# Expert layer of a decoder block: half of the experts read as fetched rows, the other half as dense, unsplit tiles

## The chip, the cores and the metric

The kernel runs on one core of one Trainium2 chip. The metric is the device time of one execution in microseconds (us). The kernel before takes 1032.59 us, the median of three runs (1030.81, 1032.59 and 1033.53).

## What is computed

The program is one decoder layer over 256 tokens of 1024 numbers in float32: a conditioning product, a projection, sparse attention beside a short convolution, an output projection, and then the part that the change touches, a retrieval layer over 16,384 single-neuron experts. Its reference, cut to what matters (8 heads, 128 keys in each half, 16 chosen pairs in each head):

```python
q = (hb @ peer_wq).reshape(B, Q_BLOCK, PEER_HEADS, 2, PEER_HALF)
s = einsum('bqhpd,hpnd->bqhpn', q, peer_subkeys)
vals, idx = top_k(s, 16)
combo = vals[..., 0, :, None] + vals[..., 1, None, :]
ids = idx[..., 0, :, None] * 128 + idx[..., 1, None, :]
top_s, pos = top_k(combo, 16)
expert = take_along_axis(ids, pos)
g = softmax(top_s)
a = gelu(einsum('bqhkd,bqd->bqhk', peer_u[expert], hb))
out = einsum('bqhk,bqhkd->bqd', g * a, peer_v[expert])
```

So each token has 128 chosen experts (8 heads by 16), each with a row of 1024 numbers in `peer_u` and one in `peer_v`. An expert's number is i * 128 + j, with i and j the two key positions. Among the 32,768 pairs that the reference's inputs give, 16,030 (49%) have j of 64 or more.

## The kernel before

Everything up to the second norm (attention, convolution, output projection) comes first and is not touched. The expert part follows in four stages.

**Queries.** Sixteen weight tiles of 512 KB go through PE against the normed tokens, held as `h2h` and `h2l`. Float32 accuracy is had by splitting: `split` (L116 to L118) rounds a tile on ScalarE to `hi`, and VectorE subtracts to get `lo`; `mm3` (L120 to L123) then adds up three products. `scores` (L839 to L845) multiplies with the sub-keys, and `top16` (L811 to L830) finds the best 16 on VectorE.

**U.** The kernel is dense: it does not fetch the rows of the chosen experts, but multiplies all tokens with all 128 tiles of `peer_u` (tile j holds the 128 experts with that j), by `u_tile` (L960 to L973): 24 products of 256 columns per tile. ScalarE takes the gelu of each result into a buffer `B0` or `B1`, which holds expert by token. During the first 64 tiles VectorE works through the generator `retrieve` (L805 to L953), which turns scores into the chosen pairs `Ti`, `Tj` and their weights `Tg`.

**G.** During the second 64 tiles `g_tile` (L975 to L995) makes, for four tokens at a time, a one-hot matrix of i on ScalarE (L981, L984) and a weighted one-hot matrix of j on VectorE (L982), multiplies them on PE (L986), and multiplies the result into the buffers (L993). Pairs that were not chosen get the weight zero.

**V.** `v_tile` (L1020 to L1023) multiplies the 128 buffered weight slices, split again, with the 128 split tiles of `peer_v`: 12 products of 512 columns per tile. `finish` (L1025 to L1030) applies the gate, adds the residual and stores.

All tiles come through one queue on SP: `load` (L110), `pump`, `advance`, `fill`, `take`. The engines' own orders come from the order in which the code emits instructions; VectorE's order in the U stage is by budget: after each tile the generator is run until the sum of its yielded estimates passes 1.38 us (L1002 to L1006). Tiles in `FULL` (L38) are taken unsplit: PE multiplies them as plain float32, in two instructions per product (L632, L643).

Of the kernel before, what the change touches and what calls it, by code (L numbers as in the profile page):

```python
# [8 lines left out]
F32 = mybir.dt.float32  # L9
# [26 lines left out]
# Order of the work. Streamed tiles are counted in the order in which they are used.  # L36
# [10 lines left out]
J0 = 64  # L47


def layout(a):  # L50
    """Only moves data: transposes, slices and repeats of the inputs."""
# [31 lines left out]
    o["pu"] = a["peer_u"].reshape(128, 128, KD, 128).transpose(1, 3, 2, 0)  # L83
# [8 lines left out]
def body(tc, i, out):  # L92
# [48 lines left out]
    def advance():  # L141
# [6 lines left out]
        if count[0] in FULL:  # L148
            ahead.append((raw,))
            return  # L150
# [93 lines left out]
    def fold(col, acc, g):  # L244
        """Adds the sums of half of acc over its partitions to a column vector."""
# [23 lines left out]
    def normed(tb):  # L269
        """x times its reciprocal root mean square, tokens on partitions."""  # L270
# [52 lines left out]
    W += [(i["pu"][j].rearrange("p k c -> p (k c)"), None) for j in range(NJ)]  # L323
# [12 lines left out]
    for j in range(NJ):  # L336
        if j >= 16 and j % 8 == 0 and j < 80:
            k = (j - 16) // 8
            queue.append((i["w_ada"][5, k], add_row(gate2, k)))
        queue.append((i["pv"][j], None))  # L340
# [454 lines left out]
    B0 = pool("B0").tile([128, NJ // 2, L], F32, name="B0")  # L795
    tr = pool("tr")
    gw = pool("gw", 2)
    Ti = tr.tile([128, L], F32, name="Ti")
    Tj = tr.tile([128, L], F32, name="Tj")
    Tg = tr.tile([128, L], F32, name="Tg")  # L800
    p2 = ExitStack()
    r1 = p2.enter_context(tc.tile_pool(name="r1", bufs=1))
    r2 = p2.enter_context(tc.tile_pool(name="r2", bufs=2))

    def retrieve():  # L805
        skT = r1.tile([128, 16, 128], F32, name="skT")
        nc.scalar.dma_start(out=skT, in_=i["sk"])
        v16 = [r1.tile([128, 16, 16], F32, name=f"v16{tb}") for tb in range(NT)]
        x16 = [r1.tile([128, 16, 16], U32, name=f"x16{tb}") for tb in range(NT)]

        def top16(items, tag):  # L811
            """items: (values, sorted values out, positions out); chains run side by side."""
            ws = []
            for c, v, x in items:
                nc.vector.max(out=v[:, 0:8], in_=c)
            yield 0.4
            for c, v, x in items:
                nc.vector.max_index(out=x[:, 0:8], in_max=v[:, 0:8], in_values=c)
            yield 0.4
            for n, (c, v, x) in enumerate(items):  # L820
                w = r2.tile([128, c.shape[-1]], F32, name=f"{tag}{n}")
                nc.vector.match_replace(out=w, in_to_replace=v[:, 0:8], in_values=c, imm_value=NEG)
                ws.append(w)
            yield 0.4
            for w, (c, v, x) in zip(ws, items):
                nc.vector.max(out=v[:, 8:16], in_=w)
            yield 0.4
            for w, (c, v, x) in zip(ws, items):
                nc.vector.max_index(out=x[:, 8:16], in_max=v[:, 8:16], in_values=w)
            yield 0.4  # L830

        def stage1(hp, sg):
            return top16([(sg[:, tb], v16[tb][:, hp], x16[tb][:, hp]) for tb in range(NT)], "wv")

        def ready():
            while todo:
                yield from stage1(*todo.pop(0))

        def scores(hp, pqT):  # L839
            ps = p_acc.tile([128, NT, 128], F32, name="acc")  # L840
            for tb in range(NT):
                nc.tensor.matmul(ps[:, tb], pqT[:, tb * 128:tb * 128 + 128], skT[:, hp], start=True, stop=True)  # L842
            sg = r2.tile([128, NT, 128], F32, name="sg", bufs=10)
            nc.scalar.copy(sg, ps)
            todo.append((hp, sg))  # L845

        todo = []
        prev = None
        cur = iter(())
        left = 0.0  # L850
        for hp in range(16):
# [9 lines left out]
            nc.scalar.copy(prev, ps)  # L861
            if hp > 2:
                left += BUDGET1
# [9 lines left out]
        yield 0  # L873
        yield from cur
        yield from ready()
        TB = range(NT)
        vv = [v16[tb].rearrange("p (h z) k -> p h z k", z=2) for tb in TB]
        xf = [r1.tile([128, 16, 16], F32, name=f"xf{tb}") for tb in TB]
        xv = [z.rearrange("p (h z) k -> p h z k", z=2) for z in xf]
        for tb in TB:  # L880
            nc.vector.tensor_copy(xf[tb], x16[tb])
# [42 lines left out]
        for tb in TB:  # L924
            for h in range(H):
                for k in range(16):
# [4 lines left out]
                    if k % 2:  # L931
                        yield 0.37
# [140 lines left out]
```

## Time and profile before

| | |
|---|---|
| runs (us) | 1030.81, 1032.59, 1033.53; median 1032.59 |
| span of the profiled execution | 1031.9 us (its own time is not listed beside the three) |
| PE busy | 991.0 us (96%) |
| VectorE (DVE) busy | 774.2 us (75%) |
| ScalarE (ACT) busy | 595.9 us (58%) |
| GpSimd (POOL) busy | 7.5 us (1%) |
| read from memory | 189.58 MB, 185 GB/s over the span |

The profile's page gives busy time per engine, the span in 40 slices, the chain of work that ended last, and the costliest groups. A busy PE is no proof of PE at its peak, since its instructions overlap: the pace is read from the starts of consecutive instructions. Other views (windows, timeline, groups by shape, DMA issues) cut the same execution into parts.

### The profile page before, as it was taken

The numbers are of one execution on the slowest core, as the hardware profiler recorded it, in microseconds if no ns is written. First come the engines' busy times: TensorE is split into PE (matmuls) and PEld (weight loads), VectorE is DVE, ScalarE is ACT, GpSimd is POOL, SyncE is SP. The second block draws the span as 40 slices with busy tenths as digits, with TensorE's granted clock in tenths as the row PEclk, the third lists the DMA queues.
The fourth block names the chain that finished last, engine by engine and source line by source line (L and its number), as shares of the span: only waits on it lengthen the run. The fifth ranks groups of instructions, "written<-read, shape, count | busy, mean of one in ns | idle before, by whom it ended". The sixth has DMA issues, their size and how long they took to land.

```text
span 1031.9 us, 18401 instructions
## 1 busy us (share of the span) xinstructions
PE 991.0 (96%) x6642; PEld 912.4 (88%) x6642; DVE 774.2 (75%) x2103; ACT 595.9 (58%) x1210; POOL 7.5 (1%) x20
## 2 busy tenths in 40 slices
PE   2599989999999999999999999999999999999998
PEld 2599987899999999999999999988888888888886
DVE  5789687788988999777788888866666666665655
ACT  3354643545445454599888888845454455455452
POOL 1000000000000000000000000000000000000000
PEclk9799998999999999999999999999999999999999
DMA  9686486345655655544444444456677777665663
GB/s 317 223 311 222 171 277 211 98 144 155 181 183 176 190 180 185 184 144 134 141 138 143 144 143 136 136 180 207 214 216 218 210 223 222 202 189 180 198 191 121
DMA packets 52891, 191.82 MB, mean 186 GB/s; under 512 B 6112, under 2 KB 6144, under 8 KB 52672
## 3 DMA queue, kind: packets, MB, share of 16 engines
q1 hardware_dynamic: 52416, 189.30, 58.4%
q8 instruction: 52, 0.85, 0.3%
q10 hardware_dynamic: 144, 1.05, 0.3%
q0 software_dynamic: 240, 0.31, 0.1%
q14 instruction: 39, 0.32, 0.1%
HBM read 189.58 MB, written 1.05 MB: 185 GB/s over the span
## 4 chain that ended last, share of the span: by engine, by line
PE 93%; DVE 4%; DMA 1%; ACT 1%; issue 0%; SPq 0%; ACTq 0%; DVEq 0%
PE acc L121 14%; PE acc L123 14%; PE acc L122 14%; PE mm L121 13%; PE mm L122 13%; PE mm L123 13%; PE pg L986 6%; PE acc L632 2%; DMA raw<-in_w_ada_dram 1%; DVE gate L219 1%; PE acc L842 1%; PE pg L517 1%; DVE acc L219 0%; PE mm L708 0%; ACT hi L117 0%
## 5 line engine op out<-in xcount | busy, mean ns | idle before, releaser
L118 DVE TENSOR_TENSOR lo<-raw,hi 128x1024 fp32r<-128x1024 f32 x302 | 369.1, 1223 | 122.7 <-ACT hi L117 120.3
L117 ACT CAST hi<-raw 128x1024 fp32r<-128x1024 f32 x302 | 316.0, 1047 | 158.1 <-PE mm L122 105.3
L121 PE MATMUL mm<-h2h,hi 128*128 128x256 f32 x1152 | 333.0, 289 | 0.5 <-ACT hi L117 0.4
L122 PE MATMUL mm<-h2l,hi 128*128 128x256 f32 x1152 | 325.9, 283 | 0.0
L123 PE MATMUL mm<-h2h,lo 128*128 128x256 f32 x1152 | 325.8, 283 | 0.0
L121 PEld LDWEIGHTS mm<-h2h,hi 128*128 128x128 f32 x1152 | 220.7, 192 | 0.9 <-ACT hi L117 0.9
L122 PEld LDWEIGHTS mm<-h2l,hi 128*128 128x128 f32 x1152 | 221.0, 192 | 0.0
L123 PEld LDWEIGHTS mm<-h2h,lo 128*128 128x128 f32 x1152 | 220.5, 191 | 0.0
L121 PE MATMUL acc<-hi,wh 128*128 128x512 f32 x512 | 199.7, 390 | 0.0
L123 PE MATMUL acc<-hi,wl 128*128 128x512 f32 x512 | 199.3, 389 | 0.0
L122 PE MATMUL acc<-lo,wh 128*128 128x512 f32 x512 | 199.3, 389 | 0.0
L117 ACT CAST wh<-B 128x256 fp32r<-128x256 f32 x128 | 52.0, 407 | 148.4 <-PE acc L122 145.6
L122 PEld LDWEIGHTS acc<-lo,wh 128*128 128x128 f32 x512 | 96.1, 188 | 20.1 <-issue 0.2
L123 PEld LDWEIGHTS acc<-hi,wl 128*128 128x128 f32 x512 | 96.1, 188 | 20.0
L121 PEld LDWEIGHTS acc<-hi,wh 128*128 128x128 f32 x512 | 96.1, 188 | 20.0 <-issue 0.2
L118 DVE TENSOR_TENSOR wl<-B,wh 128x256 fp32r<-128x256 f32 x128 | 54.2, 424 | 52.4 <-ACT wh L117 51.8
L981 ACT ACTIVATE oi<-iota,Ti 128x128 f32<-128x128 f32 x256 | 88.0, 403 | 0.0
L993 DVE TENSOR_TENSOR B<-pg,B 128x256 f32<-128x256 f32 (+63 forms) x127 | 45.0, 355 | 46.3 <-PE pg L986 46.3
L982 DVE TENSOR_SCALAR oj<-iota,Tj,Tg 128x128 f32<-128x128 f32 x256 | 71.3, 342 | 1.6 <-PE pg L986 1.6
L986 PE MATMUL pg<-oj,oi 128*128 128x128 f32 x512 | 67.6, 275 | 0.0
L986 PEld LDWEIGHTS pg<-oj,oi 128*128 128x128 f32 x512 | 62.8, 192 | 0.0
L928 DVE SCALAR_TENSOR_TENSOR ju<-iota,tf,ce 128x50 f32<-128x50 f32 x256 | 51.7, 266 | 0.0
(220 smaller groups left out, 945.9 us busy)
## 6 DMA issues: line engine op xcount, KB each, us to landing
raw<-in_pu_dram SPq DMA_DIRECT2D x128, 512.0 KB, 3.7
raw<-in_pv_dram SPq DMA_DIRECT2D x128, 512.0 KB, 4.3
raw<-in_w_ada_dram SPq DMA_DIRECT2D x48, 512.0 KB, 5.0
raw<-in_wq_dram SPq DMA_DIRECT2D x16, 512.0 KB, 3.7
raw<-in_w_c_dram SPq DMA_DIRECT2D x12, 512.0 KB, 4.7
raw<-in_w_kv_dram SPq DMA_DIRECT2D x8, 512.0 KB, 5.9
raw<-in_w_out_dram SPq DMA_DIRECT2D x8, 512.0 KB, 5.0
raw<-in_w_iq_dram SPq DMA_DIRECT2D x4, 512.0 KB, 4.8
```

Source lines behind the costliest of these rows:

```text
L117: nc.scalar.copy(hi, src)
L118: nc.vector.tensor_tensor(lo, src, hi.bitcast(F32), op=OP.subtract)
L121: nc.tensor.matmul(ps, a[0], b[0], start=first, stop=False)
L122: nc.tensor.matmul(ps, a[0], b[1], start=False, stop=False)
L123: nc.tensor.matmul(ps, a[1], b[0], start=False, stop=last)
L219: nc.vector.scalar_tensor_tensor(acc[:, s], raw[:, s], sc[:, k:k + 1], acc[:, s], op0=OP.mult, op1=OP.add)
L632: nc.tensor.matmul(ps[0], w[0][:, s], hT[:, k], start=k == 0, stop=k == KD - 1)
L928: nc.vector.scalar_tensor_tensor(ju, iota[:, :NC2], tf[tb][:, h, k:k + 1], ce[tb][:, h], op0=OP.is_equal, op1=OP.mult, accum_out=ef[tb][:, ...
L981: nc.scalar.activation(out=oi[:, n], in_=iota, func=AF.Square, bias=Ti[:, t:t + 1])
L982: nc.vector.tensor_scalar(oj[:, n], iota, Tj[:, t:t + 1], Tg[:, t:t + 1], op0=OP.is_equal, op1=OP.mult)
L986: nc.tensor.matmul(ps[:, n], oi[:, n], oj[:, n], start=True, stop=True)
L993: nc.vector.tensor_tensor(B[:, :m, t], pv[:, j0:j0 + m], B[:, :m, t], op=OP.mult)
```

## The change

Experts with j below 64 stay dense (64 tiles of U, 64 of V), but their tiles are no longer split: PE multiplies the raw float32 tile with one product where there were three. Experts with j of 64 or more are handled by fetched rows.

- `retrieve` now runs for one half of the tokens at a time (tb 0, then tb 1). The look-up of the expert number, 256 small instructions (L928), becomes, for each head, a comparison of 128x800, a product (on GpSimd for tb 0, on VectorE for tb 1) and a sum. It also writes two lists of row numbers, `iu` and `iv`; 65536 is added for pairs with j below 64, which puts them out of bounds, so that their row is not fetched.
- `fetch_u` has GpSimd fetch, for one pair slot of 128 tokens, the 128 rows of `peer_u` (4 KB each); six fetches are kept ahead. `dots` multiplies them with the tokens' own rows and sums, one VectorE instruction over 1024 columns per slot: 256 in all. `weigh` takes the gelu and the weight, `place` puts the result, transposed, on the diagonals of `S`.
- `fetch_v` has GpSimd fetch the 128 chosen rows of `peer_v` for each of four tokens (a quad); two quads are held. `strips` multiplies a quad with its 32-column parts of `S`, four products side by side in four column strips of PE, for each half of the output: 64 quads, 512 products. They add to the same sums as the dense `v_tile`.
- The order is by budget again: 3.5 us of VectorE work are emitted after each dense tile, 1.75 after each quad. By these estimates the lists for tb 0 stand after dense U tile 12, those for tb 1 after tile 48; 46 of the 64 G groups fall among the U tiles and 18 behind them; 48 of the 256 dots are emitted before V; the first quad follows dense V tile 32, one quad then follows each V tile, and 32 quads are left when the dense tiles are through.

The diff, cut to its core:

```diff
+WHOLE = set(FULL) | set(range(53, 53 + 2 * J0))
+SKIP = 65536.0
+U_US, V_US, S_US, G_US = 3.5, 3.5, 1.75, 1.0
-        if count[0] in FULL:
+        if count[0] in WHOLE:
             ahead.append((raw,))
             return
+            for z in (h, h + 1):
+                eng = nc.gpsimd if tb == 0 else nc.vector
+                eq = r2.tile([128, 16, NC2], F32, name="eq", bufs=3)
+                nc.vector.tensor_tensor(eq, iota[...], tf[...], op=OP.is_equal)
+                eng.tensor_tensor(eq, eq, ce[:, z, None].to_broadcast([128, 16, NC2]), op=OP.mult)
+                pend.append((ef[:, z], eq))
+                yield from summed(2)
+        nc.vector.tensor_scalar(off, fi[:, 1], float(J0), SKIP, op0=OP.is_lt, op1=OP.mult)
+        nc.vector.tensor_tensor(off, off, flat(ef), op=OP.add)
+        nc.vector.tensor_copy(iu[tb], off)
+    def fetch_u():
...
+                raw = pp.tile([128, D], F32, name="ug", tag=tag)
+                nc.gpsimd.indirect_dma_start(
+                    out=raw, out_offset=None, in_=i["ur"],
+                    in_offset=bass.IndirectOffsetOnAxis(ap=iu[tb][:, n:n + 1], axis=0),
+                    bounds_check=128 * 128 - 1, oob_is_err=False)
+    def dots():
...
+        nc.vector.tensor_tensor_reduce(out=junk, in0=raw, in1=h2r[:, tb], scale=1.0, scalar=0.0,
+                                       op0=OP.mult, op1=OP.add, accum_out=ad[tb][:, n:n + 1])
+        fetch_u()
+    def stream():
...
+        yield from retrieve(0)
+        other = retrieve(1)
+        for n in range(128):
+            yield dots()
+            for _ in range(2):
+                z = next(other, None)
...
+        weigh(0)
+        for n in range(128):
+            yield dots()
+        weigh(1)
+    def u_tile(j):
...
-            mm3(ps, (w[0][:, s], w[1][:, s]), (h2h[:, k], h2l[:, k]), k == 0, k == KD - 1)
+            nc.tensor.matmul(ps, w[0][:, k * 128:k * 128 + 128], h2f[:, k], start=k == 0, stop=k == KD - 1)
+    for j in range(J0):
+        ps = u_tile(j)
...
+        g_step()
+        run(U_US)
+    while spread[0] < L:
+        g_step()
+        run(G_US)
+    S = vs.tile([128, 4, 1024], F32, name="S")
+    nc.gpsimd.memset(S, 0.0)
+    for _ in range(6):
+        nc.gpsimd.memset(vg.tile([128, D], F32, name="vg"), 0.0)
+    def fetch_v():
...
+        for q in range(4):
+            t = q * 32 + n % 32
+            nc.gpsimd.indirect_dma_start(
+                out=rows[q], out_offset=None, in_=i["pv"].rearrange("j p d -> (j p) d"),
+                in_offset=bass.IndirectOffsetOnAxis(ap=iv[tb][:, t:t + 1], axis=0),
+                bounds_check=128 * 128 - 1, oob_is_err=False)
+    def strips():
...
+        for d in range(2):
+            for q in range(4):
+                nc.tensor.matmul(po[tb][d][q * 32:q * 32 + 32], S[:, q, c:c + 32], rows[q][:, d * 512:d * 512 + 512],
+                                 start=False, stop=not parts[tb], tile_position=(0, q * 32))
+        fetch_v()
+    while j < J0 or n < 64:
+        if j < J0:
+            v_tile(j)
+            j += 1
+            run(V_US)
...
+            if ("G", tb) in state and n % 32 == 0:
+                place(tb)
+            if state.get(("W", tb)):
+                strips()
+                n += 1
+                run(S_US)
```

## Rows read from the trace of the kernel before

**Rows 1.** The page: busy time of the engines over the span.
```profile
PE 991.0 (96%) x6642; PEld 912.4 (88%) x6642; DVE 774.2 (75%) x2103; ACT 595.9 (58%) x1210; POOL 7.5 (1%) x20
```

**Rows 2.** The page: the chain that ended last, by engine.
```profile
PE 93%; DVE 4%; DMA 1%; ACT 1%; issue 0%; SPq 0%; ACTq 0%; DVEq 0%
```

**Rows 3.** Windows by stage: busy us and instructions, clock, DMA share, GB/s.
```profile
252.00:436.00 184.00, 183.94 (x1533) 183.55 (x1532) 163.60 (x874) 92.99 (x149) 0.00 (x0) 1.00 0.59 181
436.00:674.00 238.00, 238.00 (x2025) 238.00 (x2024) 191.03 (x498) 209.62 (x562) 0.00 (x0) 1.00 0.46 141
681.00:1027.00 346.00, 345.94 (x1523) 285.52 (x1521) 217.30 (x265) 172.35 (x251) 0.00 (x0) 1.00 0.66 200
```

**Rows 4.** Timeline of PE: end of the queries, a split tile, its pace.
```profile
251.17 0.71 PE L842 MATMUL acc<-skT,pqT 128*128 128x128 f32 x4
...
252.08 0.28 PE L121 MATMUL mm<-h2h,hi 128*128 128x256 f32 x1
252.20 0.28 PE L122 MATMUL mm<-h2l,hi 128*128 128x256 f32 x1
```

**Rows 5.** Timeline of PE: row-half products, then an unsplit float32 tile.
```profile
111.75 0.70 PE L491 MATMUL pg<-kT,qT 64*128 64x256 f32 x4
112.28 0.60 PE L491 MATMUL mm<-kT,qT 64*128 64x256 f32 x4
112.81 3.72 PE L632 MATMUL acc<-hT,raw 128*128 128x256 f32 x16
116.18 0.47 PE L121 MATMUL acc<-h1h,hi 128*128 128x256 f32 x1
```

**Rows 6.** The chain in order of time: one G group on PE.
```profile
503.73 0.89 PE pg L986 x8
```

**Rows 7.** Groups by shape: busy us, mean ns of one, idle before.
```profile
L981 ACT ACTIVATE oi<-iota,Ti 128x128 f32<-128x128 f32 x256 | 88.0, 403 | 0.0
L984 ACT ACTIVATE oi<-oi 128x512 f32<-128x512 f32 x64 | 40.5, 632 | 1.7
L118 DVE TENSOR_TENSOR lo<-raw,hi 128x1024 fp32r<-128x1024 f32 x302 | 369.1, 1223 | 122.7 <-ACT hi L117 120.3
L118 DVE TENSOR_TENSOR wl<-B,wh 128x256 fp32r<-128x256 f32 x128 | 54.2, 424 | 52.4 <-ACT wh L117 51.8 <-PE acc L121 0.5
L928 DVE DVE_READ_ACCUMULATOR ju<-iota,tf,ce 128x1 f32 x256 | 20.9, 81 | 0.0
L253 DVE TENSOR_REDUCE fs<-mm 128x4 f32<-128x512 f32 x8 | 5.5, 688 | 2.1 <-PE mm L249 2.1
L818 DVE FIND_INDEX8 x<-v,sg 128x8 uint32<-128x128 f32 x32 | 8.7, 285 | 0.0
L818 DVE FIND_INDEX8 tx<-tv,cv 128x8 uint32<-128x50 f32 x16 | 3.1, 204 | 0.0
L1028 DVE TENSOR_TENSOR raw<-acc,gate 128x512 f32<-128x512 f32 x4 | 2.8, 692 | 0.7 <-PE acc L123 0.7
```

**Rows 8.** Timeline of POOL: its DMA issues and a fill of 128x1024.
```profile
1.45 0.71 POOL L205 DMA_DIRECT2D cols<-in_cols_dram  x1
2.15 0.97 POOL L207 MEMSET gate<- 128x1024 f32 x1
3.43 0.51 POOL L208 DMA_DIRECT2D gate<-in_b_gate_dram  x1 [0.30 <-POOL gate L207]
5.01 0.54 POOL L214 DMA_DIRECT2D aow<-in_aow_dram  x1
```

**Rows 9.** DMA issues: size of one and us from issue to landing.
```profile
raw<-in_pu_dram SPq DMA_DIRECT2D x128, 512.0 KB, 3.7
out_dram<-raw SPq DMA_DIRECT2D x4, 256.0 KB, 2.0
aow<-in_aow_dram POOLq DMA_DIRECT2D x1, 256.0 KB, 6.9
```

**Rows 10.** Windows early in the run (columns as in rows 3).
```profile
30.00:35.00 5.00, 0.00 (x0) 0.00 (x0) 3.71 (x3) 0.00 (x0) 0.00 (x0) 0.50 0.93 343
50.00:60.00 10.00, 10.00 (x86) 9.87 (x84) 6.57 (x6) 5.73 (x10) 0.00 (x0) 1.00 1.02 399
```

More of the change, by code (lines that the diff above doesn't have):

```diff
@@ L335, in body @@
     assert not ada
[L336 to L339, printed above, removed]
+    for j in range(J0):
+        if j in ROWS:
+            queue.append((i["w_ada"][5, ROWS.index(j)], add_row(gate2, ROWS.index(j))))
         queue.append((i["pv"][j], None))
@@ L803, in body @@
     r2 = p2.enter_context(tc.tile_pool(name="r2", bufs=2))
[L805 to L847, printed above, removed]
@@ new lines, in body, with rows_of_h2 @@
+    nc.gpsimd.tensor_tensor(h2f, h2h.bitcast(F32), h2l.bitcast(F32), op=OP.add)
+    def rows_of_h2(tb):
+        for g in range(2):
+            pt = p_g.tile([128, 4, 128], F32, name="pg")
+            for z in range(4):
+                nc.tensor.transpose(pt[:, z], h2f[:, g * 4 + z, TS[tb]], ident)
+            nc.scalar.copy(h2r[:, tb, g * 512:g * 512 + 512], pt)
+    skT = r1.tile([128, 16, 128], F32, name="skT")
+    nc.scalar.dma_start(out=skT, in_=i["sk"])
+    v16 = [r1.tile([128, 16, 16], F32, name=f"v16{tb}") for tb in TB]
@@ L848, in retrieve @@
         prev = None
-        cur = iter(())
         left = 0.0
@@ new lines, in place @@
+    def place(tb):
+        pt = p_mm.tile([128, 128], F32, name="mm")
+        nc.tensor.transpose(pt, state.pop(("G", tb)), ident)
+        nc.scalar.copy(S[:, :, ::33], pt.rearrange("p (q n) -> p q n", n=32))
+        state["W", tb] = True
+    def stream():
+        yield from cur
+        while todo:
+            yield from stage1(*todo.pop(0))
+        yield from retrieve(0)
[4 more added lines that the diff above has]
+                z = next(other, None)
+                if z is not None:
+                    yield z
+        for z in other:
+            yield z
+        weigh(0)
+        yield 0.3
+        for n in range(128):
+            yield dots()
+        weigh(1)
+        yield 0.3
@@ L961, in u_tile, with run @@
+    state.clear()
+    queries()
+    junk = keep.tile([128, D], F32, name="junk", tag="h2h")
+    gen = stream()
+    spent = [0.0]
+    def run(us):
+        spent[0] += us
+        while spent[0] > 0:
+            z = next(gen, None)
+            if z is None:
+                spent[0] = 0.0
+                return
+            spent[0] -= z
+    evicted = [0]
+    spread = [0]
+    stage = [None, None]
+    groups = [0]
+    def u_tile(j):
         w = take()
@@ new lines, in body @@
+    po = [[p_acc.tile([128, 512], F32, name="acc") for _ in range(2)] for _ in range(NT)]
+    quads = []
+    parts = [J0 + 32, J0 + 32]
+    def fetch_v():
+        n = state.setdefault("quad", 0)
+        if n == 64:
+            return
+        state["quad"] += 1
+        tb = n // 32
+        rows = [vg.tile([128, D], F32, name="vg") for _ in range(2 + n % 2 * 2)]
+        if n % 2 == 0:
+            two = keep.tile([128, 2, D], F32, name="two", tag="h2l")
+            rows += [two[:, q] for q in range(2)]
+        for q in range(4):
[4 more added lines that the diff above has]
+                bounds_check=128 * 128 - 1, oob_is_err=False)
+        quads.append((n, rows))
@@ new lines, in strips, with v_tile @@
+    def strips():
+        n, rows = quads.pop(0)
+        tb = n // 32
+        c = n % 32 * 32
+        parts[tb] -= 1
+        for d in range(2):
[3 more added lines that the diff above has]
+        fetch_v()
+    def v_tile(j):
+        v = take()
+        fill(min(AHEAD, J0 - 1 - j))
+        for tb in TB:
+            parts[tb] -= 1
+            for d in range(2):
+                nc.tensor.matmul(po[tb][d], B0[:, j, TS[tb]], v[0][:, d * 512:d * 512 + 512],
+                                 start=j == 0, stop=not parts[tb])
@@ L1055, in body @@
+    for tb in TB:
+        for d in range(2):
+            finish(tb, d)
+    order.close()
     ctx.close()
```

364 lines of the change are left out of this document (211 added, 153 removed).

## The prediction

> **What bounds the kernel now.** I read the page first, then the chain, then windows cut at the stages, then the timelines for the pace of single products. PE is busy for 96% of the span [rows 1] and makes up 93% of the chain that ended last [rows 2]. The windows tell where [rows 3]: from 252 us, where the last query tile ends [rows 4], PE is full through the first 64 U tiles (184 us), the other 64 with their G groups (238 us) and V (346 us), at the full clock of 2.4 GHz. VectorE and ScalarE lie beside it, the DMA engines are half to two thirds used, GpSimd does nothing. So some 780 of 1032 us are dense products whose pace is the array's. The change cuts these products in half and brings in two workers whose pace the old trace hardly shows: GpSimd, which must issue 512 fetches, and the column strips.
>
> **Before the lists are known.** A split product of 256 columns starts every 0.12 us [rows 4], so a split tile is 24 x 0.12 = 2.9 us. An unsplit one is 16 instructions and takes 116.18 - 112.81 = 3.4 us [rows 5]. Each remaining dense tile thus gets 0.5 us dearer on PE; what is saved is that there are 64 and not 128 of each kind, and that splitting leaves VectorE (1.22 us a tile [rows 7]) and ScalarE.
>
> Up to 252 us nothing changes. The token rows need 16 transposes among the queries, taken at 2 us of PE: 254.
>
> U: 64 x 3.4 = 218 us. The 46 G groups among them have half the columns of the old group's 0.89 us [rows 6]; between 0.45 (columns decide) and 0.89 (weight loads decide) I take the middle, 0.67, so 31 us. PE also meets a new wait: the transposes of the lists for tb 0 stand behind U tile 12, which PE leaves at 254 + 13 x 3.4 = 298 us. VectorE has by then 34 steps of the first search left (two instructions of 0.29 us each [rows 7]: 20 us) and the list itself: eight searches of five steps of 0.2 us (with their value loads 9 us), eight comparisons and eight sums over 800 columns, each some 1.0 us by the slope of the two subtractions in [rows 7] and by the reduction's 0.69 for 512 (16 us), some thirty short instructions (8 us). It gets there at 254 + 53 = 307, so PE waits 9 us, with all later tiles queued behind it. End of U: 254 + 218 + 31 + 9 = 512.
>
> The 18 G groups behind U have no tile to hide under. ScalarE needs 4 x 0.40 + 0.63 = 2.24 us for each [rows 7]; 40 us, to 552.
>
> V, first part: 32 tiles are 109 us of PE, but quads can't begin before the first half's gelu, and 80 of its dots are still to come. A dot costs the two-input pass over 1024 columns, 1.22, and the read of the accumulator, 0.08 [rows 7]: 104 us. GpSimd first clears 10,240 columns for S and the row buffers, at 0.97 us per 1024 [rows 8], with fetches queued behind: 10 us. So 552 + 114 + 3 (gelu, weight, transpose) = 669 us.
>
> **The alternating part.** 32 times PE does one V tile and one quad, VectorE four dots, GpSimd eight fetches (four of each table); the DMA engines bring a tile and eight half-filled fetches, 0.52 + 8 x 0.256 = 2.58 MB.
>
> - PE: 3.4 plus a quad. A quad is 16 instructions of 0.42 us; one after another 6.8, four at a time 1.7. The nearest row is the pair of row halves: eight instructions of 0.21 in 112.81 - 111.75 = 1.06 us [rows 5], where one at a time takes 1.7 and perfect pairing 0.84, a quarter over perfect. I take 2.0, so 5.4 in all.
> - VectorE: 4 x 1.30 = 5.2.
> - DMA: the fastest stretch moves 399 GB/s [rows 10]: 6.4.
> - GpSimd: 8 x p, where p is its time for one fetch. No row shows one. A plain DMA holds it for 0.51 to 0.71 us, almost whatever its size [rows 8]; a fetch must also read 128 numbers, check each and form each address. Bounds: 0.53, if that is free, and 1.42, twice the dearest issue, if a list costs a second pass. I take the middle, 1.0: 8.0 us.
>
> The largest counts, since each worker waits for the others within two quads or six rows: 32 x 8.0 = 256, to 925; 3 us for the second gelu.
>
> For memory the Trainium skill states another limit ("DMA: Bandwidth & Descriptors", Specifications): about 358 GB/s per core, which would make a turn 7.2 us and would decide if fetches were cheap; the trace's 399 [rows 10] speaks against it as a hard limit.
>
> **The tail.** 32 quads remain with nothing beside them. Two are held: the fetches of quad n+2 start when quad n is done. A cycle of 4p, landing and product serves two quads. Landing took 2.0 us for 256 KB and 3.7 for 512 KB on SP's queue, 6.9 on GpSimd's in the crowded start [rows 9]; I take 3. So (4.0 + 3 + 2.0) / 2 = 4.5 us a quad, 144 us, to 1072. With 2.0 it is 16 us less, with 6.9 62 more. Last come four instructions of 0.69 [rows 7] and a store of 2.0: 1077. The span of before is 0.7 us under its median: 1078, or 4% slower. In general, 758 + 320 p.
>
> Of the strips the Trainium skill says ("TensorEngine Tiling (Array Packing)", Theoretical Speedup and Key Properties) that parts of up to 32 columns run up to four times as fast, and that changing the mode drains the array. By its factor alone a quad is 1.7 us, and the sum 1073; the trace's pair of row halves fell short of perfect.
>
> **Rivals.**
>
> 1. *Fetches are cheap: faster.* If p is as for the dearest plain issue, 0.71, the DMA engines decide the alternating part, 32 x 6.4 = 206, and the tail is 32 x (2.8 + 5) / 2 = 125: 669 + 206 + 3 + 125 + 6 = 1009; with 0.53, 998. It decides from p = 0.86 down. For it: one row or 128, the issue costs the same [rows 8], so descriptors by the hundred are cheap. Against: none of those reads a list.
> 2. *The strips run one after another.* Then a quad is 7.0, PE decides both parts: 32 x 10.4 + 32 x 7.0 = 557, and the sum is 1235. Two at a time, it is only the tail that grows: 1104. Against the first: the row halves did overlap [rows 5].
> 3. *The change doesn't do what it says: out-of-bounds rows are fetched too.* Twice the bytes, 4.7 MB a turn, 11.8 us; with the tail at 5.5: 669 + 377 + 3 + 176 + 6 = 1231. Nothing in the trace speaks to it.
>
> A second upward cost inside the forecast: PE works 2 of 4.5 us in the tail. In a stretch without products the granted clock stood at 0.50, 1.2 GHz [rows 10]; at that level a quad takes 4.0 and the tail 32 us more.
>
> **How the numbers follow.** The forecast (p from about 0.86 to 1.42, strips side by side) gets 0.55; rival 1, 0.38, because p's lower bound is nearer to what rows show; rival 2, 0.04; rival 3, 0.03. A measurement of this kernel can tell about 0.3% (3 us) from no change: that is p between 0.85 and 0.87, 0.03, taken from rival 1. So faster 0.35, same 0.03, slower 0.62. The time is the forecast's, 1078. The upper bound of p gives 758 + 454, and 12 more since the issue then fills the tail: 1224; the lower gives 998. I cut 1 in 10 at either end by stopping at 990, under the cheap fetch, and 1205, at a p of about 1.4. The forecast's own range is 1036 to 1205.
>
> **What would show it.** Right: GpSimd's issues fill nearly every microsecond of the alternating part, PE shows gaps before the strips that end with fetched rows, the tail is 130 to 170 us. The fetch's duration on GpSimd's timeline settles between forecast and rival 1; the starts of the eight strip products settle rival 2; bytes on the software queue (about 131 MB, or 268) settle rival 3. U should end near 512, with a wait of PE near 300 us, and the first quad start near 669. The prediction is wrong if GpSimd idles in the alternating part, or if PE is full to the end.

## The result, and the profile after

The changed kernel takes 1244.14 us, the median of four runs (1241.85 to 1248.80), the kernel before 1033.0 us beside it: a ratio of 1.205 with a 95% interval of 1.202 to 1.208. Slower was forecast, but by 4% and not by 20%, and the time lies above the range. The profiled execution took 1244.16 us, with a span of 1242.5 us; all that follows is measured against it.

The page of the changed kernel: busy time per engine (to hold against [rows 1]), the software queue, which carries the fetches, and the chain that ended last by engine ([rows 2]).

```profile
PE 1045.6 (84%) x4614; PEld 618.7 (50%) x4614; DVE 704.8 (57%) x1703; ACT 283.3 (23%) x739; POOL 587.1 (47%) x548
...
q0 software_dynamic: 73968, 131.79, 36.2%
...
PE 35%; issue 24%; DMA 13%; DVE 11%; POOL 10%; another core or an unknown queue 4%; ACT 1%; POOLq 1%; SPq 0%; DVEq 0%; ACTq 0%
```

PE made up 93% of the chain and is now 35% of it; no engine has taken its place for the whole span. GpSimd is busy for 47%, which looks harmless as an average. The windows by stage (columns as in [rows 3]: PE, weight loads, VectorE, ScalarE, GpSimd, clock, DMA share, GB/s) show where it isn't. They are U, the G groups behind it, V up to the first quad, the part in which V tiles and quads alternate, and the tail:

```profile
258.30:526.90 268.60, 264.65 (x1410) 237.31 (x1409) 204.61 (x709) 133.78 (x414) 79.75 (x63) 1.00 0.56 178
526.90:568.60 41.70, 31.89 (x136) 30.06 (x136) 28.20 (x85) 29.35 (x79) 13.92 (x15) 0.50 0.19 56
568.60:690.50 121.90, 112.85 (x263) 48.91 (x262) 100.34 (x164) 0.70 (x2) 91.59 (x80) 0.96 0.89 301
690.50:1056.50 366.00, 280.49 (x777) 76.54 (x781) 168.86 (x269) 1.87 (x4) 270.52 (x251) 0.92 0.75 230
1056.50:1237.50 181.00, 138.00 (x512) 25.09 (x504) 1.75 (x3) 0.00 (x0) 118.71 (x120) 0.98 0.62 173
```

Against the stages forecast (512, 552, 669, 925 and 1072 us) the first three come 15, 17 and 21 us late, the alternating part takes 366 us instead of 256, and the tail 181 instead of 144. So 147 of the 166 us of error lie in the two parts that have quads. In the alternating part GpSimd handles 251 fetches in 366 us, one in 1.46 us, and in the tail the remaining 120 at nearly the same pace.

GpSimd's groups in the alternating part (count, busy us, mean ns of one, idle time before them and what ended it), and then its timeline for a few us of it (start, duration, and the idle time before in brackets):

```profile
L1009 POOL DMA_INDIRECT ug<-in_ur_dram,iu x123 | 126.2, 1026 | 37.5 <-issue 34.1 <-DMA vg<-in_pv_dram,iv 1.5 <-DMA two<-in_pv_dram,iv 0.9
L1175 POOL DMA_INDIRECT vg<-in_pv_dram,iv x96 | 111.4, 1161 | 47.6 <-issue 22.8 <-remote 11.4 <-PE acc L1188 11.2
L1175 POOL DMA_INDIRECT two<-in_pv_dram,iv x32 | 33.5, 1046 | 10.6 <-issue 8.2 <-remote 1.1 <-DMA ug<-in_ur_dram,iu 0.6
```

```profile
980.35 0.99 POOL L1175 DMA_INDIRECT two<-in_pv_dram,iv  x1 [0.30 <-issue]
981.64 0.99 POOL L1175 DMA_INDIRECT two<-in_pv_dram,iv  x1 [0.30 <-issue]
982.94 0.99 POOL L1009 DMA_INDIRECT ug<-in_ur_dram,iu  x1 [0.30 <-issue]
984.23 0.99 POOL L1009 DMA_INDIRECT ug<-in_ur_dram,iu  x1 [0.30 <-DMA vg<-in_pv_dram,iv]
```

A fetch holds GpSimd for 0.99 us, almost exactly the price that was taken. But behind each one stand 0.30 us in which the engine waits for nothing that the profile shows, so the next begins 1.29 us after it. For 251 fetches that is 324 us; 23 us more come from fetches that took longer (the mean is 1.08 us), and some 20 us from waits for buffers. The longer ones go mostly with VectorE's dots: in the tail, where VectorE is idle, the mean is 0.99 us, and in e10_no_dots, which has no dots, it is 0.99 to 1.01 us in the whole run. A plain issue had a gap of 0.30 us ahead of it too [rows 8], put down there to a fill that ended.

PE's longest waits of the whole span end with fetched rows. The list of waits (us in total, times, longest) begins with two lines of rows and, between them, one of time in which PE waited for nothing that the profile shows:

```profile
PE acc L1188 <- DMA vg<-in_pv_dram,iv: 69.7, 74, 5.1
PE acc L1188 <- issue: 31.7, 34, 3.6
PE acc L1188 <- DMA two<-in_pv_dram,iv: 17.9, 21, 2.4
```

Where rows are there, the strips run side by side. In the timeline of PE just behind the first quad, the 16 instructions of the second take less than two us between two V tiles:

```profile
694.04 3.70 PE L1198 MATMUL acc<-raw,B 128*128 128x512 f32 x8
697.67 1.92 PE L1188 MATMUL acc<-vg,S 128*32 128x512 f32 x16
699.53 3.70 PE L1198 MATMUL acc<-raw,B 128*128 128x512 f32 x8
```

Where they aren't, the two instructions of one strip run alone and take 1.04 us:

```profile
850.23 1.04 PE L1188 MATMUL acc<-vg,S 128*32 128x512 f32 x2 [0.91 <-DMA vg<-in_pv_dram,iv]
```

So PE counts as busy for 277 us from the first quad to the last dense tile (690.5 to 1047.5 us), while e2_no_v needs 180 for the same products: the busy share hides part of the waiting.

### The profile page after: what moved, and what is told of

It is laid out like the page before. It is cut to its first block, busy times and chain, and to the rows that moved or that the text cites. A ratio compares the mean times of both kernels' runs of the same rounds, so it can differ in the third digit from the quotient of the medians.

```text
span 1242.5 us, 14277 instructions
## 1 busy us (share of the span) xinstructions
PE 1045.6 (84%) x4614; PEld 618.7 (50%) x4614; DVE 704.8 (57%) x1703; ACT 283.3 (23%) x739; POOL 587.1 (47%) x548
## 2 busy tenths in 40 slices
DMA packets 108170, 255.92 MB, mean 206 GB/s; under 512 B 45732, under 2 KB 45764, under 8 KB 107968
## 3 DMA queue, kind: packets, MB, share of 16 engines
q0 software_dynamic: 73968, 131.79, 36.2%
HBM read 390.90 MB, written 1.05 MB: 315 GB/s over the span
## 4 chain that ended last, share of the span: by engine, by line
PE 35%; issue 24%; DMA 13%; DVE 11%; POOL 10%; another core or an unknown queue 4%; ACT 1%; POOLq 1%; SPq 0%; DVEq 0%; ACTq 0%
PE mm L1085 14%; POOL vg L1175 5%; DMA ug<-in_ur_dram,iu 5%; DMA vg<-in_pv_dram,iv 4%; PE pg L1119 3%; PE acc L1188 3%; POOL ug L1009 3%; DVE junk L1020 3%; PE acc L126 2%; PE acc L128 2%; PE acc L127 2%; DMA two<-in_pv_dram,iv 2%; POOL two L1175 2%; DMA raw<-in_w_ada_dram 2%
## 5 line engine op out<-in xcount | busy, mean ns | idle before, releaser
L1020 DVE CUSTOM_DVE_ANT_0 junk<-ug,h2r 128x1024 f32<-128x1024 f32 x256 | 313.4, 1224 | 193.8 <-DMA ug<-in_ur_dram,iu 135.4
L1009 POOL DMA_INDIRECT ug<-in_ur_dram,iu x256 | 279.6, 1092 | 255.8 <-DVE ad L1020 159.9
L1188 PE MATMUL acc<-vg,S 128*32 128x512 f32 x768 | 255.1, 662 | 102.3 <-DMA vg<-in_pv_dram,iv 69.7
L1175 POOL DMA_INDIRECT vg<-in_pv_dram,iv x192 | 206.4, 1075 | 96.8 <-issue 43.6
L1198 PE MATMUL acc<-raw,B 128*128 128x512 f32 x512 | 235.0, 611 | 1.4 <-issue 1.2
L1085 PE MATMUL mm<-h2f,raw 128*128 128x256 f32 x1024 | 231.4, 381 | 0.0
L1085 PEld LDWEIGHTS mm<-h2f,raw 128*128 128x128 f32 x1024 | 190.9, 190 | 24.0
L1188 PE MATMUL acc<-two,S 128*32 128x512 f32 x256 | 99.4, 688 | 22.2 <-DMA two<-in_pv_dram,iv 17.9
L1119 PE MATMUL pg<-oj,oi 128*128 128x64 f32 x512 | 79.2, 310 | 11.2 <-DVE oj L1129 7.6
L123 DVE TENSOR_TENSOR lo<-raw,hi 128x1024 fp32r<-128x1024 f32 x46 | 60.5, 1319 | 33.0 <-ACT hi L122 32.8
L122 ACT CAST hi<-raw 128x1024 fp32r<-128x1024 f32 x46 | 47.8, 1046 | 18.3 <-DMA raw<-in_w_kv_dram 4.9
L1097 DVE TENSOR_TENSOR B<-B,ge 128x128 f32<-128x128 f32 (+44 forms) x49 | 12.6, 256 | 52.7 <-ACT ge L1096 43.8
```

The source lines that it names most:

```text
L122: nc.scalar.copy(hi, src)
L123: nc.vector.tensor_tensor(lo, src, hi.bitcast(F32), op=OP.subtract)
L1009: nc.gpsimd.indirect_dma_start(out=raw, out_offset=None, in_=i["ur"], in_offset=bass.IndirectOffsetOnAxis(ap=iu[tb][:, n:n + 1], axis=0), ...
L1020: nc.vector.tensor_tensor_reduce(out=junk, in0=raw, in1=h2r[:, tb], scale=1.0, scalar=0.0, op0=OP.mult, op1=OP.add, accum_out=ad[tb][:, n: ...
L1085: nc.tensor.matmul(ps, w[0][:, k * 128:k * 128 + 128], h2f[:, k], start=k == 0, stop=k == KD - 1)
L1119: nc.tensor.matmul(ps[:, n], oi[:, n], oj[:, n], start=True, stop=True)
```

## The experiments

The theory behind the first runs: the time behind the first quad is the number of fetches times GpSimd's price for one, gap included. Rivals: the bytes that they bring, the strips, and, later, the dots on VectorE. Beside the first four the kernel before took 1033.9 us, beside the next four 1032.1 us, beside the others 1031.6 and 1033.4 us. All but e7_u_only have one time each, so that only differences of several per cent are read from them.

### Few bytes: e1_narrow

```diff
-                    out=raw, out_offset=None, in_=i["ur"],
+                    out=raw[:, :64], out_offset=None, in_=i["ur"].rearrange("n (b d) -> (n b) d", d=64),
...
-                out=rows[q], out_offset=None, in_=i["pv"].rearrange("j p d -> (j p) d"),
+                out=rows[q][:, :64], out_offset=None, in_=i["pv"].rearrange("j p (b d) -> (j p b) d", d=64),
```

> The same 512 fetches, each of 64 numbers a row (256 B) and not 1024; the dots and products repeat those 64 (the rest of each row is left out). Theory 'issue' (GpSimd's 1.09 us a fetch and the 0.3 us between two are the bound): the span stays at 1200 to 1245 us, the part with quads at 10.3 to 11.4 us a turn and the tail at 5.2 to 5.7 us a quad. Theory 'bytes' (memory and DMA engines are the bound): PE's own time remains, 7.1 us a turn and 3.4 to 4 a quad, and the span falls to about 1045 us. Theory 'strips' (PE's slow strips are the bound): no change in either part.

Measured: 1200.25 us. The software queue moves 8.68 MB instead of 131.79, 7% of the bytes, and 44 of 1244 us go with them. GpSimd is busy for 583.7 us, as before (587.1). From the first quad at 681.8 us to the last at 1192.6 us it handles 369 fetches, one in 1.38 us (windows up to the last dense tile, and behind it, columns as above):

```profile
681.80:1022.40 340.60, 264.68 (x767) 77.94 (x768) 157.60 (x249) 0.00 (x0) 265.10 (x241) 0.90 0.25 71
1022.40:1192.60 170.20, 145.74 (x519) 26.41 (x517) 5.67 (x10) 1.59 (x4) 128.62 (x128) 0.99 0.09 16
```

It is the count that costs, and hardly the bytes.

### No fetches for the second table: e2_no_v

```diff
+        if n >= 2:
+            quads.append((n, held[n % 2]))
+            return
...
+        held.append(rows)
```

> The fetches of the second table are left out but for the first two quads, whose rows all later quads multiply; the 256 of the first table stay. Theories 'issue' and 'bytes' alike: what is left in a turn is PE, 3.4 for a dense tile, 3.4 for a quad (two strips at a time, as the trace's 16 products in 3.4 us) and 0.3, so 7.1 us a turn and 3.4 a quad in the tail: 690 + 227 + 3 + 109 + 5 = 1034 us. Theory 'strips': 11 us a turn stay, span near 1240.

Measured: 951.35 us, below what was expected. The first quad starts at 689.4 us as in the changed kernel (690.5); then a turn, counted to the end of the dense tiles, takes 5.9 us instead of 11.2, and the tail's quads 1.8 us each (32 in 57 us): strips that wait for nothing run four at a time. PE binds the turns here, with 180 of 189 us:

```profile
689.00:878.00 189.00, 180.12 (x767) 60.91 (x768) 159.53 (x253) 0.34 (x1) 139.55 (x122) 0.97 0.82 267
```

The expectation was too high because it had taken 3.4 us for a quad, read from the first one at 690 us. That one ran behind a wait of 8.3 us, at a granted clock of 0.50 (1.2 GHz), with 1.07 us for an instruction where the later ones take 0.6.

### All rows fetched: e3_in_range

```diff
-SKIP = 65536.0
+SKIP = 0.0
```

> Pairs with j below 64 are not sent out of bounds, so all 128 rows of each fetch arrive (268 MB on the software queue and not 132). Theory 'issue': within 2% of 1243 us, unless the DMA engines now fill, 4.7 MB a turn at 400 GB/s being 11.8 us. Theory 'bytes': a turn grows to some 15.7 us and a quad of the tail to 7.0 at the 300 GB/s of the stretch before the first quad: about 1420 us.

Measured: 1278.93 us, 3% more than the changed kernel, for 268.77 MB on the software queue instead of 131.79. Rows that are out of bounds are thus not fetched in the changed kernel, and leaving them out saves little. Some 28 of the 35 us lie ahead of the first quad, which starts at 718.1 us. From there to the end of the dense tiles it takes 367 us with 249 fetches, one in 1.47 us, where the changed kernel takes 357 with 245, one in 1.46. The DMA engines are full there, at 406 GB/s in the mean of the 367 us:

```profile
718.00:1085.00 367.00, 288.69 (x767) 73.54 (x768) 164.78 (x261) 0.05 (x1) 269.94 (x249) 0.92 1.02 406
```

### Plain transfers in their place: e4_plain

```diff
-                nc.gpsimd.indirect_dma_start(
-                    out=raw, out_offset=None, in_=i["ur"],
-                    in_offset=bass.IndirectOffsetOnAxis(ap=iu[tb][:, n:n + 1], axis=0),
-                    bounds_check=128 * 128 - 1, oob_is_err=False)
+                r0 = (tb * 64 + n // 2) * 128
+                nc.gpsimd.dma_start(out=raw[:, :512], in_=i["ur"][r0:r0 + 128, :512])
...
+            nc.gpsimd.dma_start(out=rows[q][:, :512], in_=i["pv"][(n * 4 + q) % 128][:, :512])
```

> Each fetch becomes a plain DMA of GpSimd's of the same 256 KB (128 rows of 512 numbers, in order, without a list; the values are not the experts'). Theory 'issue': a plain issue holds GpSimd for 0.54 and 0.3 between two, 0.84: 6.7 us a turn, under PE's 7.1, and (3.4 + 3 + 3.4) / 2 = 4.9 a quad: about 690 + 227 + 3 + 157 + 5 = 1080 us. Theory 'bytes': the span stays near 1243 us.

Measured: 1043.66 us, 200 us below the changed kernel, with the same number of transfers, about the same bytes and the same strips and dots. GpSimd's busy time falls to 309.1 us, 0.54 us for a transfer, the duration in [rows 8], and its timeline has three of them in 1.89 us, so that one starts 0.67 us after the other:

```profile
853.78 1.89 POOL L1010 DMA_DIRECT2D ug<-in_ur_dram  x3
```

Reading a list thus makes an issue 0.62 us dearer, from one start to the next, 512 times. From the first quad to the end of the dense tiles GpSimd is no longer the bound, but PE (220 of 227 us) and the DMA engines (share 1.00, 373 GB/s) are both full, and no run tells which of the two binds:

```profile
680.00:907.00 227.00, 220.41 (x768) 69.20 (x769) 158.73 (x251) 0.25 (x1) 133.10 (x249) 1.00 1.00 373
```

### No fetches for the first table: e5_no_u

```diff
+                if len(held) == 6:
+                    fetched.append((tb, n, held[n % 6]))
+                    return
```

> After the first six, the fetches of the first table are left out: the dots read the six rows that lie there (their sums are not those of the reference), and all 256 fetches of the second table stay. If the time is the number of fetches on GpSimd at 1.43 us each, 250 fewer leave 256 x 1.43 = 366 us from the first quad to the end; the first quad itself comes earlier, since the dots wait for nothing but VectorE (between 620 and 690 us), and the time is 1000 to 1065 us, with one quad in 5.7 us both in the part with V tiles and behind it. If the fetches of one table were hidden behind those of the other or behind PE (rival: the strips with their reading of rows bound the second half), the turns stay above 10 us and the time above 1200 us.

Measured: 1057.02 us, in the expected range. The first quad starts at 671.8 us. In the tail 122 fetches take 179 us, 1.47 us each. The alternating part takes 6.2 us a quad, not the 5.7 that the pace of the fetches would allow: 198 us for 32 turns, PE busy for 192 of them.

```profile
671.80:869.80 198.00, 191.89 (x767) 64.10 (x768) 158.19 (x249) 0.31 (x1) 136.85 (x127) 1.00 0.83 265
```

So with half the fetches the bound passes from GpSimd to PE there.

### Half the list: e6_half_lists

```diff
-                    in_offset=bass.IndirectOffsetOnAxis(ap=iu[tb][:, n:n + 1], axis=0),
+                    in_offset=bass.IndirectOffsetOnAxis(ap=iu[tb][:64, n:n + 1], axis=0),
...
-                in_offset=bass.IndirectOffsetOnAxis(ap=iv[tb][:, t:t + 1], axis=0),
+                in_offset=bass.IndirectOffsetOnAxis(ap=iv[tb][:64, t:t + 1], axis=0),
```

> Every fetch keeps its place, but its list has the first 64 of the 128 entries, and sums and strips read those 64 rows alone (the other 64 pairs of each token are left out); 512 fetches as before. If a fetch has one price whatever its list, the bytes halve and the time is that of the kernel with narrow rows, 1190 to 1215 us, with 0.99 us for one fetch. If GpSimd works entry by entry, the busy time of one falls to between 0.5 us (all of it by entries) and 0.77 us (only what it has above the 0.54 us of a plain transfer), a fetch comes every 0.8 to 1.07 us with the gap of 0.30 us, a turn of 8 takes 6.4 to 8.6 us, and the time is 1010 to 1110 us.

Measured: 1249.05 us, neither of the two times, but the price of one fetch answers the question. The timeline of GpSimd:

```profile
831.02 0.94 POOL L1009 DMA_INDIRECT ug<-in_ur_dram,iu  x1 [0.30 <-issue]
832.27 0.94 POOL L1009 DMA_INDIRECT ug<-in_ur_dram,iu  x1 [0.30 <-issue]
```

64 entries cost 0.94 us where 128 cost 0.99: less than a thousandth of a us per entry, and the rest belongs to the fetch as such. The time doesn't fall to that of e1_narrow because TensorE ran at a lower granted clock behind the first quad: 0.80 in the alternating part (0.92 in the changed kernel) and 0.52 in the tail (0.98), near the lower level of 1.2 GHz, where an instruction of the strips takes 1.06 us (0.62). Its products there run over 64 partitions; why the clock stayed low isn't shown.

### Without the bound: e8_no_bound

```diff
-                    in_offset=bass.IndirectOffsetOnAxis(ap=iu[tb][:, n:n + 1], axis=0),
-                    bounds_check=128 * 128 - 1, oob_is_err=False)
+                    in_offset=bass.IndirectOffsetOnAxis(ap=iu[tb][:, n:n + 1], axis=0))
```

It starts from e1_narrow, with the same edit at the second table and SKIP = 0.

> The kernel with narrow rows (64 numbers) once more, but with all indices in range and without the bound that a fetch checks them against (the sums are not those of the reference). If the 0.30 us between two fetches are the setting of that bound, they go, a fetch comes every 1.0 to 1.1 us, and the 1200 us fall by 80 to 150 us to 1050 to 1120 us. If the gap belongs to every fetch, the time stays at 1190 to 1210 us and the trace shows 0.30 us between two fetches as before.

Measured: 1270.6 us, outside both. The gap of 0.30 us is still there, with 0.94 us for a fetch (1.00 in e1_narrow), so it isn't the setting of the bound. That the kernel is 70 us slower than e1_narrow isn't explained by that: 50 of the 70 lie ahead of the first quad (732.1 us), where PE waits 42.2 us for dense tiles of the second table, and behind it there are stretches like the one below, where GpSimd stands still for 6 us between two fetches.

```profile
831.31 0.95 POOL L1009 DMA_INDIRECT ug<-in_ur_dram,iu  x1 [0.30 <-issue]
838.28 0.94 POOL L1176 DMA_INDIRECT vg<-in_pv_dram,iv  x1 [6.02 <-issue]
839.52 0.94 POOL L1176 DMA_INDIRECT vg<-in_pv_dram,iv  x1 [0.30 <-issue]
```

### The first half of the change alone: e7_u_only, e9_u_ahead

The second table is dense for all j, and its weights for j from 64 on are spread by one-hot products (`high_step`, one for four tokens, as `g_step`).

```diff
+    def high_step():
...
+                nc.vector.tensor_scalar(oj[:, n], iota[:, J0:], Tj[:, t:t + 1], Tw[:, t:t + 1],
+                                        op0=OP.is_equal, op1=OP.mult)
...
+                    mm3(po[tb][d], (wh[:, TS[tb]], wl[:, TS[tb]]), (v[0][:, s], v[1][:, s]), j == 0, j == NJ - 1)
```

> Only the first half of the change: the dots of the pairs with j>=64 from fetched rows, but no fetch of the second table. Their weights are spread over j 64 to 127 by one-hot products as those of j<64 are, and the second table is dense for all 128 j, unsplit for the first 68 and split behind, as the kernel before has it; nothing of the computation is left out. With 256 fetches instead of 512, the issue theory has them end near 823 us (some 78 by 568 us, 178 x 1.43 us behind), PE is done with j<64 at 568 + 64 x 3.5 = 792 us, the rest of the one-hot products takes 30 us, and 64 more tiles at 2.7 us 173 us: 1010 to 1045 us, within 2% of the kernel before. If what makes the changed kernel slow were its first half (dots on VectorE, unsplit tiles on PE), this kernel would be slower than before by 50 us or more.

Measured: 1435.1 us, a ratio of 1.391 to the kernel before (1.386 to 1.395). The expectation failed by 390 us, through two waits that were mine and not the change's. The 60 split tiles took 6.84 us each, since `fill` split the next tile (which waits for PE) ahead of the B that PE waited for; and the last dot came at 936 us, not 823, as the written order gave VectorE too few dots for a tile of PE. PE's waits in the split tiles add up to 118 us; the granted clock there was 0.76, so that the products took longer too. e9_u_ahead takes both waits out:

```diff
-        v = take()
-        fill(min(AHEAD, NJ - 1 - j))
+        v = take()
...
+            split(wh, wl, B)
+        fill(min(AHEAD, NJ - 1 - j))
...
-U_US, V_US, S_US, G_US = 3.5, 3.5, 1.75, 1.0
+U_US, V_US, S_US, G_US = 4.0, 6.0, 1.75, 1.0
```

> e7_u_only once more, with two waits of its own taken out: B of a tile is split ahead of the next tiles of the table instead of behind them, and the order gives VectorE more dots for each tile of PE. The 60 split tiles of the second table then take 2.7 to 3.2 us instead of 6.84 us (220 to 250 us less), and the last dot comes at 860 to 900 us instead of 936 us: 1110 to 1190 us. So the first half of the change alone still ends behind the kernel before, because its 256 fetches start late and the one-hot products of j>=64 wait for the last of them. If it were the waits of e7 alone that made it slow, the time would fall below 1040 us.

Measured: 1127.59 us, within the range; the split tiles now take 2.7 us at a clock of 1.00. Its windows from the end of the G groups on: dots of fetched rows beside V, one-hot products, split tiles of V.

```profile
569.00:880.00 311.00, 227.32 (x732) 118.04 (x731) 269.49 (x542) 91.45 (x294) 204.86 (x178) 0.86 0.77 245
880.00:960.00 80.00, 77.01 (x330) 47.01 (x329) 28.22 (x96) 55.33 (x168) 0.00 (x0) 1.00 0.40 127
960.00:1120.00 160.00, 158.98 (x702) 131.30 (x700) 91.67 (x120) 76.48 (x113) 0.00 (x0) 1.00 0.57 182
```

From 569 us on 178 of the 256 fetches are still to come, and the last is issued at 844.6 us, one in 1.55 us; PE has only 227 us of work in 311. The kernel before is through with U at 674 us [rows 3]. PE's busy time over the whole run, 982.7 us, is even below that of before (991.0), so what half of the change loses is idle time, 84 us of it in the first of these windows. The fetches alone are not shown to be the reason: VectorE is busy for 269 of the 311 us, with some 20 us of waits ahead of its dots, and GpSimd with its gaps for 258 of the 276 us up to the last fetch. Either would nearly fill the stretch.

### The dots and the order: e10_no_dots, e11_budgets, e12_no_dots_narrow

```diff
-        nc.vector.tensor_tensor_reduce(out=junk, in0=raw, in1=h2r[:, tb], scale=1.0, scalar=0.0,
-                                       op0=OP.mult, op1=OP.add, accum_out=ad[tb][:, n:n + 1])
```

> The changed kernel with all 512 fetches and without the sums on VectorE over the fetched rows (their values are set to 0). This tells the two parts of its time apart. If VectorE sets when the first quad can start and GpSimd's issue sets the pace behind it, the first quad comes at 590 to 650 us instead of 690 us, but a turn of 8 fetches still takes 10.4 to 11.4 us and a quad of the tail 5.2 to 5.7 us: 1110 to 1200 us. If the sums on VectorE bound the turns, these fall to the 5.4 us that PE needs, and the time falls below 1000 us. If neither depends on them, the time stays within 15 us of 1244 us.

Measured: 1377.7 us, 134 us slower with less work, which no theory had. The turns are 10.9 us (836 to 1185 us) and the quads of the tail 5.6, as the issue theory has them: without the sums on VectorE the part with quads goes as before. But the first quad starts at 836 us. In two stretches before it, PE's instructions came one by one; its timeline there, and its waits from 258 to 720 us:

```profile
576.38 0.59 PE L1085 MATMUL mm<-h2f,raw 128*128 128x256 f32 x1 [2.92 <-issue]
579.17 0.58 PE L1085 MATMUL mm<-h2f,raw 128*128 128x256 f32 x1 [2.20 <-issue]
581.97 0.59 PE L1085 MATMUL mm<-h2f,raw 128*128 128x256 f32 x1 [2.21 <-issue]
```

```profile
PE mm L1085 <- issue: 83.2, 48, 2.9
PE pg L1119 <- issue: 50.0, 26, 3.2
```

133 us in which PE waited for nothing that the profile shows, while GpSimd issued a fetch every 1.29 us (nothing on VectorE slowed it down there). The narrow form of the same kernel (e1_narrow's edit and e10_no_dots' together) tells whether the rows' traffic has to do with it:

> e10_no_dots with rows of 64 numbers instead of 1024 (the sums are left out, and products have a row's first 64 numbers again and again): the same 512 fetches as densely issued, with hardly any bytes. In e10 TensorE started one instruction in about 1.4 us, waiting for nothing that the trace shows, as long as fetches followed one another without a break. If the traffic of the rows holds up its instructions, that goes with the bytes: the first quad comes at 590 to 650 us and the time is 1080 to 1170 us. If it goes with the fetches themselves, whatever they bring, the first quad stays within 30 us of 836 us and the time above 1300 us.

Measured: 1170.68 us. These waits of PE are gone, all 133 us of them. The first quad comes at 672.4 us, later than expected (and the time lies just past the end of its range): as in e5_no_u and in the changed kernel, 32 V tiles stand ahead of it, here at 3.5 us each from 559.7 us on. So the written order (a quad may start when the generator has passed all dots of the first half) holds the first quad back even where no dot does. In the changed kernel the same 32 tiles end at 681.2 us, and PE then waits 8.3 us more for the last dot. From the first quad on, 370 fetches take 491 us in e12_no_dots_narrow, 1.33 us each, the nearest to the bare 1.29 us of all runs.

The order is the only thing that e11_budgets changes:

```diff
-U_US, V_US, S_US, G_US = 3.5, 3.5, 1.75, 1.0
+U_US, V_US, S_US, G_US = 4.2, 5.0, 2.0, 2.0
```

> The changed kernel with the hand-paced order changed alone: 4.2, 5.0, 2.0 and 2.0 us of VectorE's work for a U tile, a V tile, a quad and a G step instead of 3.5, 3.5, 1.75 and 1.0 us. If the late first quad is a matter of that order, it comes 20 to 50 us earlier, and the time is 1190 to 1225 us; the pace of one fetch in 1.4 to 1.46 us behind it does not change. If the fetches bound from the first one on, the time stays at 1235 to 1255 us.

Measured: 1207.56 us, as expected. The first quad starts at 649.5 us, 41 us earlier. Only 13 V tiles stand ahead of it now, PE is through with them at 610.5 us, and then it stands still ahead of the product that transposes the weights of the first half:

```profile
PE mm L1034 <- issue: 38.1, 1, 38.1
```

In that wait VectorE works off the last dots, whose rows come one in 1.3 us. So with the earlier order it is the dots that set the first quad. From there 372 fetches take 550 us, 1.48 us each, as in the changed kernel (1.47). This is the fastest form of the whole change here, and still 17% behind the kernel before. No run that computes everything beats that one; e2_no_v's 951 us lack the second table's rows.

## Why the prediction was wrong

**The failed step is the price of a fetch**: "I take the middle, 1.0: 8.0 us". The mechanism was the right one, and GpSimd's busy time for one fetch (0.99 us when nothing is in the way, 1.08 in the mean) was what I took. What was missed is that the busy time isn't the price: with the gap of 0.30 us and the waits, one fetch costs 1.46 us. The formula of the prediction with that price gives 758 + 320 x 1.46 = 1225, and 13 us more since four fetches then take longer than a quad's cycle in the tail. The later first quad adds 21 us, and the two parts hold 371 fetches, not the 384 of the formula, which is 19 us less: about 1240. The price even lies above the upper bound (1.42), which was a multiple of a duration and had no term for what lies between two issues. The range was cut on that side at a price of 1.4, and so missed the time. The time alone would have spoken for rival 2 (1235) or rival 3 (1231); it is the trace that rules them out.

**What the price depends on** is shown in the main: hardly on the bytes (e1_narrow), hardly on the number of entries (e6_half_lists: 0.94 us for half of them), hardly on the bound (e8_no_bound: the same gap, 0.06 us less for the fetch); a plain transfer of like size has 0.67 us from start to start instead of 1.29 (e4_plain). That the time goes with the count is shown from both sides: without the second table's fetches 951 us, without the first's 1057. What GpSimd does in the 0.30 us isn't shown by any run.

**Rival 1** (cheap fetches, faster) fell, and e4_plain shows that even the price of plain issues would not have made the kernel faster: 1044 us, about 1% above the kernel before, and not 1009. The alternating part then takes 227 us where the rival had 206, with PE and the DMA engines both full (373 GB/s; 399 were taken). **Rival 2** fell: a quad whose rows are there takes 1.92 us, where the prediction took 2.0 and perfect overlap is 1.7. The Trainium skill's rule on column strips ("TensorEngine Tiling (Array Packing)", Theoretical Speedup), up to four times as fast, agrees with this: 6.8 / 1.92 is 3.5. **Rival 3** fell too: 131.79 MB on the software queue, as forecast (131), and 268.77 in e3_in_range. Its price was nevertheless nearly right: with all rows fetched the kernel takes 1279 us (1231 forecast), and 11.5 us a turn (11.8 forecast). The changed kernel's turn of 11.2 us comes near to that by chance, for the other reason; the bytes tell the two apart.

**The stages before.** The end of U came 15 us late: 4 from the start, an unsplit tile took 3.51 us (3.4 taken) and a G group 0.84 (0.67 taken), while the wait near 300 us was 2.5 and not 9 us. Neighbouring rows of PE's timeline show both prices as differences of starts:

```profile
400.69 1.00 PE L1119 MATMUL pg<-oj,oi 128*128 128x64 f32 x8
401.53 3.67 PE L1085 MATMUL mm<-h2f,raw 128*128 128x256 f32 x16
405.04 1.00 PE L1119 MATMUL pg<-oj,oi 128*128 128x64 f32 x8
```

The G groups behind U took 41.7 us (40 forecast), at a granted clock of 0.50 (1.2 GHz), and V up to the first quad 122 us (117). There the prediction had VectorE's dots decide, and they did, but only by the 8.3 us that PE waits behind the 32 tiles which the written order puts first:

```profile
615.09 66.06 PE L1198 MATMUL acc<-raw,B 128*128 128x512 f32 x152 [0.20 <-DMA raw<-in_pv_dram]
689.46 0.47 PE L1034 MATMUL mm<-ident,ad 128*128 128x128 f32 x1 [8.32 <-DVE ad L1020]
```

The dot itself was right: 1.22 and 0.08 us. That the sum came near was luck: the 10 us for clearing the buffers fell under the G groups (524 to 533 us), while VectorE stood idle for some 20 us between the dots, more than half of it for rows, which come no faster than one in 1.29 us. There, too, the price of a fetch was missing.

**The tail.** 4.5 us a quad was worked out from landing and products that wait for each other; measured are 5.7 us. Four fetches at 1.29 us are 5.2, and some 20 us of waits in the whole tail make up most of the rest. With the true price the issue fills the tail and the landing is nearly hidden; the cycle that the prediction had there was not what decided. The clock there is 0.98, so the 32 us kept for a lower one didn't come.

## What to carry to other kernels

Price an issue by the distance from one start to the next, not by its busy time, and when no row of the old profile has it, let the upper bound hold a gap as well: 0.3 us is nothing once and 150 us in 512 issues. Fetching only what is needed pays in bytes, but if the issuing engine is the bound the number of fetches must fall, and half-filled lists cost nearly as much as full ones. A near sum can hold two errors that cancel, and a near time can fit a rival: look at the waits and the bytes before the time is believed. In a hand-paced order, look both at what stands ahead of the first instruction of a stage and at the wait just before it: here the two ended within 9 us of each other.

## What was not expected of the hardware

- A fetch of 128 rows holds GpSimd for 0.99 us and 0.30 us more pass until the next; with 64 rows it is 0.94 us, and with rows of 64 numbers (e1_narrow) 1.00. While VectorE works on dots some fetches take up to 2.1 us: the mean is 1.08 us in the alternating part and 0.99 in the tail.
- Rows that the bound excludes still count: in the changed kernel 45,732 packets of under 512 B stand on the page, in e3_in_range 12,256. The difference, 33,476, is two for each of the 16,738 pairs with j below 64, one in each table. The page's count of bytes read from memory is 390.90 MB in both, though the queues moved 255.92 MB in the changed kernel.
- In stretches in which fetches follow one another without a break, TensorE's instructions can come late: in e10_no_dots it got one matmul in 1.4 to 2.8 us there and waited 133 us in all, and with narrow rows (e12_no_dots_narrow) not once. Bytes alone don't decide it: e8_no_bound, with 17.12 MB, shows such waits among the strips (43.8 us), and e3_in_range, with the most bytes, none among PE's longest waits before the first quad. What does decide stays open.
- The DMA engines kept up 406 GB/s for 367 us in e3_in_range. The Trainium skill gives about 358 GB/s for a core ("DMA: Bandwidth & Descriptors", Specifications), as half of what the two cores of a stack share. Here one core runs, and the measurement is above that figure, as [rows 10] already were for a short stretch.
